# Moving the start addresses of activations, h and shared K/V against the weights in a two-layer decoder trunk

## The chip, the core and the metric

The kernel runs on one core of one Trainium2 chip. The metric is device microseconds of one execution, the median of three runs. A profile is one further execution, recorded by the hardware profiler; its span, from the first to the last instruction, is a little shorter than its own device time.

## What is computed

Two layers of a decoder trunk over 256 positions of width 1024, batch 1, float32. The products that matter are these (cut from the reference):

```python
def swiglu(h, w_in, w_out):
    gu = h @ w_in
    g, u = jnp.split(gu, 2, axis=-1)
    return (jax.nn.silu(g) * u) @ w_out          # D_FF = 2816

def reference(x, c, ...):
    for layer in range(2):
        ...
        x = x + 0.5 * (1.0 + g)[:, None, :] * swiglu(h, ffn_w_in[layer, 0], ffn_w_out[layer, 0])
        ...
        # layer 0: causal pooling mixer; layer 1: block attention on shared K/V
        x = x + (1.0 + g)[:, None, :] * y
        ...
        x = x + 0.5 * (1.0 + g)[:, None, :] * swiglu(h, ffn_w_in[layer, 1], ffn_w_out[layer, 1])
        if layer == 0:
            kv = shared_kv(x, ...)
    return x
```

Ahead of each block stand an RMS norm and a shift and scale that are computed from `c` with the `ada` weights. There are four such SwiGLU blocks in all, and they hold nearly all of the multiplications.

## The kernel before

**Layout.** Channels lie on the 128 partitions, positions run along a row. `xT` holds the residual stream as 8 channel tiles of 256 positions. A float32 product is made of three TensorE matmuls in the format `F32R`: each factor is cut into a high part and the rest (`hi`, `lo` for weights, `hhi`, `hlo` for the normed input h, `acth`, `actl` for the SwiGLU activations, `hkvh`, `hkvl` for the normed input of the shared K/V), and `mm3` (L255 to L260) adds high times high (L256), high weights times low input (L259), and low weights times high input (L260):

```python
    def mm3(o, wh, wl, xh, xl, start, stop):
        i = nc.tensor.matmul(o, wh, xh, start=start, stop=False, skip_group_check=True)
        nc.tensor.matmul(o[:, 0:T], wh, xl, start=False, stop=False, skip_group_check=True)
        nc.tensor.matmul(o, wl, xh, start=False, stop=stop, skip_group_check=True)
```

Each of these loads 128 x 128 weights (the weight load, PEld in the profile, is an instruction of its own) and streams 256 columns of the other factor, the moving operand. A weight block is 512 bytes of each partition's row, a moving operand 1024 bytes. So within one tile every weight block starts at the same address modulo 512, and so does every moving operand, with one exception: the tiles `xah` and `xal` (a scaled copy of `xT` that stands in for h in the first steps of three of the blocks) and `kh`, `kl` (the keys, in the same room) have rows of 258 columns per channel tile, 1032 bytes, so that their k-th piece begins 8k bytes further on.

**Stages.** Weights stream from HBM into `raw` tiles, ScalarE makes `hi` (L168), VectorE makes `lo` (L169), TensorE uses them once. In a SwiGLU block, `gstep` makes one 128-channel piece of gate and up (48 matmuls into `gu`), `evac` turns it into `acth` and `actl`, and `ystep` multiplies these into `y` (24 matmuls for each piece). The projections of K and Q go to `pj`, those of V to `v` (where hkv is the stationary operand and the weights move), scores to `s`, the weighted values to `att`, the output projection to `y` with h as the moving operand. VectorE also makes the modulation vectors with dot products (L264).

**What sets the order.** TensorE's and SyncE's instructions stand in the order in which the program issues them, which lists of steps write out by hand (`MIXER`, `AFTER_B`, `ATTENTION`); the other engines are ordered by a scheduler.

**What sets the addresses.** Six pools are laid one behind another in each partition, in the order of their creation (L91 to L96; `pp` is in PSUM): `ax` (activations), `cp` (constants, `xT`, `mb`, and the rooms `kxhi` and `kxlo`, which hold `xah`, `xal`, `kh`, `kl`), `wp` (weights: `raw`, `hi`, `lo`), `tp` (temporaries), `hp` (h), and behind them `xp` (early tiles of ada weights) and later, in the same place, `ap` (shared K/V, q, probabilities). A tile takes its bytes rounded up to 32. Three tiles are never read or written and only take room: `room0` in `ax`, `room1` in `cp`, `room2` in `hp` (L100, L101, L110). Before, they take 64, 64 and 128 bytes per partition.

Of the kernel before, what the change touches and what calls it, by code (L numbers as in the profile page):

```python
# [7 lines left out]
F32 = mybir.dt.float32  # L8
# [5 lines left out]
P = 128  # L14
# [72 lines left out]
def trunk(ctx: ExitStack, tc: tile.TileContext, xin, cin, small, ada, kvada, win0a, win1a, win0b,  # L87
# [3 lines left out]
    ax = ctx.enter_context(tc.tile_pool(name="ax", bufs=8))  # L91
    cp = ctx.enter_context(tc.tile_pool(name="cp", bufs=1))
    wp = ctx.enter_context(tc.tile_pool(name="wp", bufs=2))
    tp = ctx.enter_context(tc.tile_pool(name="tp", bufs=2))
    hp = ctx.enter_context(tc.tile_pool(name="hp", bufs=1))
# [1 line left out]
    ctx.enter_context(tc.manual_schedule(engines=ORDERED))  # L97


    ax.tile([P, 16], F32, tag="room0", name="room0", bufs=1)  # L100
    hp.tile([P, 32], F32, tag="room2", name="room2")  # L101

    uid = [0]

# [2 lines left out]
        return f"{s}_{uid[0]}"  # L107


    cp.tile([P, 16], F32, tag="room1", name="room1")  # L110
    ident = cp.tile([P, P], F32, tag="ident", name="ident")
    ones = cp.tile([P, P], F32, tag="ones", name="ones")
    sm = cp.tile([P, C_N], F32, tag="sm", name="sm")
# [1053 lines left out]
```

## Time and profile before

| what | value |
|---|---|
| median of three runs | 892.27 us (892.19 to 893.82) |
| the profiled execution, device time | 894.87 us |
| its span | 893.0 us |
| TensorE busy in the span | 881.7 us, 99% |
| VectorE busy | 717.5 us, 80% |
| ScalarE busy | 453.3 us, 51% |
| granted TensorE clock | full (2.4 GHz) throughout |

A matmul's record lasts about 280 ns, because it runs from the start of its stream to the end of its way through the array; the next one starts long before that. So the duration says nothing of the pace. The pace is the distance from one matmul's start to the next one's, called a step here: a stretch of the trace divided by the matmuls that start in it. A count of matmuls in a window takes in those that reach over its ends, which for a record of 0.28 us is two more than start in it.

### The profile page before, as it was taken

Reading aid. Unit: us, or ns where it says so; the run is one execution under the profiler, and the core shown is the slowest. Engines: PE = TensorE matmul, PEld = TensorE weight load, DVE = VectorE, ACT = ScalarE, POOL = GpSimd, SP = SyncE. Lnnn points to the kernel's source line nnn. Section 1 sums busy time; section 2 is a strip of 40 time slices with the busy share of each in tenths; the row PEclk is TensorE's granted clock in tenths of the full one; section 3 lists DMA queues with packets and bytes.
Section 4 is the critical chain, followed back from the end, with each engine's and each line's share of the span. In section 5 each row is a group of like instructions: output and inputs, shape, how many; then the busy total and the mean of one; then the engine's idle time right before and its main releaser. Section 6 shows DMA issues by size and latency. Waiting matters only on the chain.

```text
span 893.0 us, 17812 instructions
## 1 busy us (share of the span) xinstructions
PE 881.7 (99%) x7398; PEld 875.0 (98%) x7398; DVE 717.5 (80%) x1224; ACT 453.3 (51%) x721; POOL 32.3 (4%) x41
## 2 busy tenths in 40 slices
PE   6999999999999999999999999999999999999998
PEld 4999999999999999999999999999999999999998
DVE  5988988878997888869998888779888794665553
ACT  3456444328744343547554434457676584443431
POOL 0000000002000000000000000002211100000000
PEclk9999999999999999999999999999999999999999
DMA  9987998784799998775779989754534277656421
GB/s 353 420 342 270 418 386 346 296 318 160 261 421 417 369 357 337 261 262 183 301 269 385 362 324 359 293 189 142 178 106 132 90 285 276 229 173 202 176 72 48
DMA packets 41699, 240.32 MB, mean 269 GB/s; under 512 B 4625, under 2 KB 5009, under 8 KB 20370
## 3 DMA queue, kind: packets, MB, share of 16 engines
q1 hardware_dynamic: 41618, 239.18, 71.3%
q8 instruction: 58, 0.95, 0.4%
q14 instruction: 23, 0.19, 0.1%
HBM read 238.11 MB, written 1.05 MB: 268 GB/s over the span
## 4 chain that ended last, share of the span: by engine, by line
PE 98%; DVE 1%; ACT 1%; DMA 0%; POOL 0%; issue 0%; DVEq 0%; SPq 0%; POOLq 0%
PE gu L259 18%; PE gu L260 18%; PE gu L256 18%; PE y L259 10%; PE y L260 10%; PE y L256 10%; PE pj L256 2%; PE pj L259 2%; PE pj L260 2%; PE gu L727 1%; PE v L256 1%; PE v L260 1%; PE v L259 1%; PE z L803 1%; PE hs L914 1%; DMA xT<-in_x_dram 0%
## 5 line engine op out<-in xcount | busy, mean ns | idle before, releaser
L168 ACT CAST hi<-raw 128x1024 fp32r<-128x1024 f32 (+1 forms) x322 | 302.5, 974 | 311.6 <-PE gu L259 211.7
L169 DVE TENSOR_TENSOR lo<-raw,hi 128x1024 fp32r<-128x1024 f32 (+1 forms) x322 | 354.6, 1128 | 123.6 <-ACT hi L168 120.8
L259 PE MATMUL gu<-hlo,hi 128*128 128x256 f32 x1248 | 348.6, 279 | 0.0
L260 PE MATMUL gu<-hhi,lo 128*128 128x256 f32 x1248 | 348.4, 279 | 0.0
L256 PE MATMUL gu<-hhi,hi 128*128 128x256 f32 x1248 | 347.9, 279 | 0.0
L260 PEld LDWEIGHTS gu<-hhi,lo 128*128 128x128 f32 x1248 | 234.6, 188 | 0.2 <-DVE lo L169 0.2
L256 PEld LDWEIGHTS gu<-hhi,hi 128*128 128x128 f32 x1248 | 234.6, 188 | 0.0
L259 PEld LDWEIGHTS gu<-hlo,hi 128*128 128x128 f32 x1248 | 234.5, 188 | 0.0
L259 PE MATMUL y<-actl,hi 128*128 128x256 f32 x704 | 196.7, 279 | 0.0
L260 PE MATMUL y<-acth,lo 128*128 128x256 f32 x704 | 196.5, 279 | 0.0
L256 PE MATMUL y<-acth,hi 128*128 128x256 f32 x704 | 196.1, 279 | 0.0
L256 PEld LDWEIGHTS y<-acth,hi 128*128 128x128 f32 x704 | 132.4, 188 | 0.0
L260 PEld LDWEIGHTS y<-acth,lo 128*128 128x128 f32 x704 | 132.3, 188 | 0.0
L259 PEld LDWEIGHTS y<-actl,hi 128*128 128x128 f32 x704 | 132.3, 188 | 0.0
L264 DVE CUSTOM_DVE_ANT_0 rawX<-rawX,cb 128x1024 f32<-128x1024 f32 x88 | 104.1, 1219 | 0.1
L417 ACT ACTIVATE sl<-gu 128x256 f32<-128x256 f32 x79 | 29.4, 377 | 38.3 <-PE gu L260 36.0
L129 ACT CAST acth<-sl 128x256 fp32r<-128x256 f32 x79 | 31.9, 406 | 24.4 <-DVE sl L418 22.6
L418 DVE TENSOR_TENSOR sl<-gu,sl 128x256 f32<-128x256 f32 x79 | 32.8, 418 | 12.7 <-ACT sl L417 12.7
L256 PE MATMUL gu<-xah,hi 128*128 128x258 f32 x144 | 41.3, 287 | 0.0
L260 PE MATMUL gu<-xah,lo 128*128 128x258 f32 x144 | 40.7, 283 | 0.0
L259 PE MATMUL gu<-xal,hi 128*128 128x256 f32 x144 | 40.7, 283 | 0.0
L130 DVE TENSOR_TENSOR actl<-sl,acth 128x256 fp32r<-128x256 f32 x79 | 32.9, 418 | 2.1 <-ACT acth L129 2.1
(147 smaller groups left out, 975.1 us busy)
## 6 DMA issues: line engine op xcount, KB each, us to landing
raw<-in_win1b_dram SPq DMA_DIRECT2D x57, 1024.0 KB, 5.4
raw<-in_wout_dram SPq DMA_DIRECT2D x88, 512.0 KB, 6.0
rawX<-in_ada_dram SPq DMA_DIRECT2D x38, 1024.0 KB, 8.0
raw<-in_win1a_dram SPq DMA_DIRECT2D x14, 1024.0 KB, 9.9
kxhi<-in_ada_dram SPq DMA_DIRECT2D x11, 1024.0 KB, 8.3
raw<-in_win0b_dram SPq DMA_DIRECT2D x12, 768.0 KB, 5.5
kxlo<-in_ada_dram SPq DMA_DIRECT2D x9, 1024.0 KB, 8.4
rawA<-in_ada_dram SPq DMA_DIRECT2D x9, 1024.0 KB, 7.5
```

The costliest lines, as they stand in the source:

```text
L129: i = nc.scalar.copy(hi, src)
L130: nc.vector.tensor_tensor(lo, src, hi.bitcast(F32), op=ALU.subtract)
L168: return [(lambda a=a, b=b: after_anchor(nc.scalar.copy(hi[:, a:b], raw[:, a:b])), lambda a=a, b=b: nc.vector.tensor_tensor(lo[:, a:b], ra ...
L169: lambda a=a, b=b: nc.vector.tensor_tensor(lo[:, a:b], raw[:, a:b], hi[:, a:b].bitcast(F32), op=ALU.subtract)) for a, b in cut]
L256: i = nc.tensor.matmul(o, wh, xh, start=start, stop=False, skip_group_check=True)
L259: nc.tensor.matmul(o[:, 0:T], wh, xl, start=False, stop=False, skip_group_check=True)
L260: nc.tensor.matmul(o, wl, xh, start=False, stop=stop, skip_group_check=True)
L264: i = nc.vector.tensor_tensor_reduce(out=v, in0=v, in1=cb, scale=1.0, scalar=0.0, op0=ALU.mult, op1=ALU.add, accum_out=mb[:, col:col + 1])
L417: nc.scalar.activation(sl, ps[:, 0:T], AF.Silu)
L418: nc.vector.tensor_mul(sl, ps[:, T:2 * T], sl)
L727: nc.tensor.matmul(g0[j][:, half * T:(half + 1) * T], w0[:, (2 * j + half) * P:(2 * j + half + 1) * P], h0, start=(half == 0), stop=False, ...
L803: nc.tensor.matmul(zps[g][:, t * T:(t + 1) * T], xs[:, kt, t * P:(t + 1) * P], pw[:, kt * T:(kt + 1) * T], start=(t == 0 and i == 0), stop ...
```

## The change

The three unused tiles are resized: `room0` goes, `room1` in `cp` grows from 64 to 416 bytes, `room2` in `hp` shrinks from 128 to 32.

```diff
@@ trunk
-    ax.tile([P, 16], F32, tag="room0", name="room0", bufs=1)
-    hp.tile([P, 32], F32, tag="room2", name="room2")
+    hp.tile([P, 8], F32, tag="room2", name="room2")
...
-    cp.tile([P, 16], F32, tag="room1", name="room1")
+    cp.tile([P, 104], F32, tag="room1", name="room1")
```

No instruction is added, removed or moved. In the two built programs every engine has the same instructions in the same order, with the same shapes, the same offsets inside their tiles and the same waits. What differs is where the tiles begin. `ax` moves down by 64 bytes, everything from `cp` through `tp` up by 288, `hp` and what lies behind it up by 192. The starts in each partition, modulo 512:

| tile | before | after |
|---|---|---|
| weights `hi`, `lo`, `raw` | 416 | 192 |
| activations `acth`, `actl` | 192 | 128 |
| `hhi`, `hlo`, `hkvh`, `hkvl`, `qh`, `ql`, `ph`, `pl` | 448 | 128 |
| `xah`, `kh`, piece k | 288 + 8k | 64 + 8k |
| `xal`, `kl`, piece k | 352 + 8k | 128 + 8k |

The phase of a matmul is, in what follows, the start of its moving operand less the start of its stationary one, modulo 512:

| matmuls | phase before | phase after |
|---|---|---|
| `gu` from h, `pj` from hkv and from h, `y` from h | 32 | 448 |
| `y` from the activations | 288 | 448 |
| `gu` from `xah`, piece k | 384 + 8k | 384 + 8k |
| `gu` from `xal`, piece k | 448 + 8k | 448 + 8k |
| `v` (weights move, hkv stands) | 480 | 64 |
| `s` from `kh`, head k | 352 + 8k | 448 + 8k |
| `s` from `kl`, head k | 416 + 8k | 0 + 8k |
| `att` (probabilities move, V stands) | 256 | 0 |

## Rows read from the trace of the kernel before

**Rows 1.** The page: busy us and instructions of each engine, then the chain's engines.

```profile
PE 881.7 (99%) x7398; PEld 875.0 (98%) x7398; DVE 717.5 (80%) x1224; ACT 453.3 (51%) x721; POOL 32.3 (4%) x41
...
PE 98%; DVE 1%; ACT 1%; DMA 0%; POOL 0%; issue 0%; DVEq 0%; SPq 0%; POOLq 0%
```

**Rows 2.** What TensorE waited for: us in total, times, longest.

```profile
PE cb L639 <- DMA crow<-in_c_dram: 2.3, 1, 2.3
PE rb L350 <- POOL r L344: 2.0, 1, 2.0
PE gu L727 <- ACT h L724: 1.5, 1, 1.5
PE ss L336 <- DVE sq L699: 1.2, 1, 1.2
PE att L259 <- DVE pl L130: 0.2, 1, 0.2
```

**Rows 3.** TensorE in stretches of the four SwiGLU blocks: window, length, busy (matmuls), granted clock.

```profile
40.00:200.00 160.00, 160.00 (x1374) 1.00 0.87 341
240.00:400.00 160.00, 160.00 (x1361) 1.00 0.90 349
420.00:580.00 160.00, 160.00 (x1373) 1.00 0.86 326
730.00:880.00 150.00, 150.00 (x1288) 1.00 0.53 187
```

**Rows 4.** Page and tile rows: how many matmuls of each kind there are.

```profile
L256 PE MATMUL gu<-hhi,hi 128*128 128x256 f32 x1248 | 347.9, 279 | 0.0
L256 PE MATMUL y<-acth,hi 128*128 128x256 f32 x704 | 196.1, 279 | 0.0
L256 PE MATMUL y<-hhi,hi x64: 277/280/366, 671.4 to 702.3; 128*128 128x256 f32 x64
L256 PE MATMUL pj<-hkvh,hi x64: 277/278/366, 593.9 to 625.9; 128*128 128x256 f32 x64
L256 PE MATMUL pj<-hhi,hi x64: 277/280/364, 626.2 to 660.8; 128*128 128x256 f32 x64
L256 PE MATMUL v<-hi,hkvh x64: 277/281/369, 588.2 to 668.4; 128*128 128x256 f32 x64
```

**Rows 5.** Timeline, first V step and first `pj` step behind it: start us, us.

```profile
588.20 0.28 PE L256 MATMUL v<-hi,hkvh 128*128 128x256 f32 x1
...
593.89 0.28 PE L256 MATMUL pj<-hkvh,hi 128*128 128x256 f32 x1
```

**Rows 6.** Timeline, six `att` matmuls, from the first to what follows.

```profile
661.13 0.28 PE L256 MATMUL att<-ph,acth 128*128 128x256 f32 x1
...
661.84 0.38 PE L990 MATMUL pT<-ident,p 128*128 128x128 f32 x2
```

**Rows 7.** Timeline, steps from `xah` and `xal`, pieces 0 and 1 in turn.

```profile
214.60 0.28 PE L259 MATMUL gu<-xal,hi 128*128 128x256 f32 x1
...
218.82 0.28 PE L256 MATMUL gu<-xah,hi 128*128 128x258 f32 x1
```

**Rows 8.** Chain of waits: four transposes, whose moving operand has 128 columns.

```profile
612.46 0.44 PE rbk L350 x4
```

**Rows 9.** Timeline, four steps of a K projection and the next start.

```profile
611.24 0.28 PE L256 MATMUL pj<-hkvh,hi 128*128 128x256 f32 x1
611.36 0.28 PE L259 MATMUL pj<-hkvl,hi 128*128 128x256 f32 x1
611.48 0.28 PE L260 MATMUL pj<-hkvh,lo 128*128 128x256 f32 x1
611.60 0.28 PE L256 MATMUL pj<-hkvh,hi 128*128 128x256 f32 x1
611.71 0.28 PE L259 MATMUL pj<-hkvl,hi 128*128 128x256 f32 x1
```

**Rows 10.** VectorE in the stretch that has most of it: window, length, busy.

```profile
420.00:580.00 160.00, 142.81 (x228) 1.00 0.86 326
```

**Rows 11.** VectorE's dot products by source tile: duration ns min/median/max, starts.

```profile
L264 DVE CUSTOM_DVE_ANT_0 rawX<-rawX,cb x88: 1214/1219/1226, 9.2 to 439.7; 128x1024 f32<-128x1024 f32 x88
L264 DVE CUSTOM_DVE_ANT_0 kxhi<-kxhi,cb x24: 1205/1218/1224, 260.8 to 797.5; 128x1024 f32<-128x1024 f32 x24
L264 DVE CUSTOM_DVE_ANT_0 kxlo<-kxlo,cb x22: 1207/1220/1223, 267.3 to 825.5; 128x1024 f32<-128x1024 f32 x22
```

## The prediction

> **What bounds the kernel now.** I read the page first, then what TensorE waited for, then its pace stage by stage. TensorE is busy in 99% of the span and makes 98% of the chain that ended last [rows 1]. All of its waits together are 7.2 us, and all but 0.2 of that lies in the opening, before its first long run of matmuls [rows 2]. So from then on there is one queue of matmuls that never runs dry, and the time is the number of matmuls times the distance between two starts. VectorE has 80% of the span [rows 1], 142.8 of 160 us where it has most [rows 10]; ScalarE has half. The granted clock is full in every stretch [rows 3].
>
> The pace is what the change can touch, so it has to be read finely. In three of the four SwiGLU blocks a step takes 160 us / (1374 - 2) = 116.6 ns, 160 / 1371 = 116.7 and 150 / 1286 = 116.6; in the second block it is 160 / 1359 = 117.7 ns [rows 3]. Nothing waits in any of these stretches, the shapes are equal, and the clock is equal. The V projection goes slower still: 48 steps from 588.20 to 593.89 are 118.5 ns each [rows 5]. The transposes, where the same 128 x 128 weight load goes with only 128 moving columns, come every 0.44 / 4 = 110 ns [rows 8]. So a step of 256 columns costs about 7 ns over what its weight load alone sustains, and how much over depends on something that is neither shape nor wait. What the V projection has of its own is its phase: its moving operand begins 480 bytes beyond the stationary one, not 32 or 288. Phases 32 and 288 both give 116.6.
>
> A rule of the Trainium skill speaks against all this: "TensorE: Matmul & The Clock Gate", section "Step-by-step: what each phase is for", says that weights and moving operand come through read ports of their own, so that loading the next weights takes no read bandwidth from the matmul that runs. By it the start addresses could not matter and the sum would be zero; the rows above show steps that differ by 2 ns among equal shapes, so here it does not settle the question, and it is a rival below.
>
> **The change, part by part.** *Instructions:* none is added or removed and none moves, so nothing is paid or saved there.
>
> *How many steps change their phase.* From 32 to 448: `gu` from h, three lines of 1248; `pj`, three of 64 and three of 64; the output projection, three of 64. From 288 to 448: `y` from the activations, three of 704 [rows 4]. That is 3 x (1248 + 128 + 64 + 704) = 6,432 steps, of which 1,359 lie in the stretch that runs at 117.7 and, for this sum, 5,073 at 116.6 [rows 3]. The steps from `xah` and `xal` (432) keep their phase. V (192) goes from 480 to 64, `att` (48) from 256 to 0, `s` (48) shifts; these 288 have no row at their new phase. They run at about 118.5 now; with 116.6 and 120.6 as ends, both read below, they are worth 288 x -1.9 = -0.5 to 288 x 2.1 = +0.6 us, and I take zero.
>
> *What a step costs at 448.* No row shows a run of equal steps at 448. The nearest are three. V, at 480, is 32 bytes away, and all three matmuls of an `mm3` have the one phase, as they will after the change: 118.5 ns [rows 5]. `att`, at 256, which like 448 is a multiple of 64 while 32, 288 and 480 are not: 0.71 us / 6 = 118.3 ns [rows 6]. The first steps from `xah` and `xal`, where one matmul of every six stands at exactly 448 and the rest between 384 and 456: 4.22 us / 35 = 120.6 ns, part of it because two of three stream 258 columns [rows 7]. On the other side, the transposes' 110 ns [rows 8] is the lowest that a 128 x 128 weight load has here. So the bounds are 110 and 120.6 ns. I take V's 118.5: it is nearest in phase and the only long run in which all steps share one phase that is not 32 or 288, and `att` says the same.
>
> *The sum.* 5,073 x (118.5 - 116.6) = 9.6 us, and 1,359 x (118.5 - 117.7) = 1.1 us: 10.7 us, all of it on the path, since TensorE waits for nobody and a slower TensorE finds every operand earlier. The profiled execution took 894.9 us, so 905.6 by its own time; the median of the runs shown is 2.6 below it, so 903.0 against 892.3. With 120.6 for every step it is 5,073 x 4.0 + 1,359 x 2.9 = 24.2 us: 916.5.
>
> *The other engines.* ScalarE, VectorE and the DMAs read and write at new addresses too. The rows that would show a price are the dot products, which read two tiles at once: from `rawX`, `kxhi` and `kxlo`, which lie 288, 128 and 192 bytes beyond `cb`, they take 1219, 1218 and 1220 ns [rows 11]. After the change the three lie 192, 128 and 192 beyond it. So nothing; and what there was would be covered by TensorE, which reaches its work later than it is ready. That cover is thinnest at 142.8 of 160 us [rows 10].
>
> **The rivals.**
>
> *448 is as good as 32 and 288.* These two are 256 apart and give the same 116.6 [rows 3], so a phase is not simply good or bad by its distance; 448 may be a third of that kind. For it: two of the two phases with thousands of steps agree to 0.1 ns. Against it: every other phase in the trace, 480, 256 and 384 to 504, costs more [rows 5, 6, 7]. It gives 892.3, with 1.5 us less if the second block falls into the pace of the others, 1,359 x 1.1. The rule of ports in the Trainium skill's "TensorE: Matmul & The Clock Gate", told above, would end here too.
>
> *448 is better: the side that is not slower.* The mechanism would be that the weight load's reads and the stream's reads get in each other's way for less of the step. The place is every one of the 6,432 steps; it decides at 116.4 ns, where the sum is 0.2% below. For it: in a K projection at phase 32 steps of 0.12 and of 0.11 us follow each other in a group of four that takes 0.47 us [rows 9], so single steps do get through sooner, and 110 ns is possible for the load [rows 8]. Against it: the four together are no faster than 117, and no phase in the trace holds a lower mean. Half way to 110, at 113.3, it would be 5,073 x 3.3 + 1,359 x 4.4 = 22.7 us: 869.6. All the way, at 110, it is 5,073 x 6.6 + 1,359 x 7.7 = 43.9 us: 848.4. VectorE would then have its 142.8 us in 160 x 110 / 116.6 = 151 us, tight but still not the bound.
>
> *The slow pace of the second block everywhere.* The second block's steps have the phases of the others and are 1.1 ns longer, from its beginning to its end [rows 3]: so there is a state that a run of matmuls enters and keeps. If 448 is neither better nor worse but favours that state in all blocks, it costs 5,073 x 1.1 = 5.6 us: 897.9. This is a smaller slowdown by another cause, and it shows as 117.7 instead of 118.5.
>
> *The change does not do what it says:* the start addresses follow from the tile sizes, and the phases above from them; I give this no weight.
>
> **How the numbers follow.** The forecast, a step of more than 118 ns at 448, gets 0.41; the slow pace everywhere 0.14; as good as before 0.17; better 0.28. A difference of 0.2%, 1.8 us, is about what a measurement of this kernel can tell from none; 10.7 and 5.6 us are well beyond it, so slower is 0.55, same 0.17, faster 0.28. The predicted time is 903.0. The likeliest case alone runs from 899 to 916.5. The range has to hold eight in ten: upward to 916, where all steps cost what the mixed ones do, and downward through the rival that is better to about its half-way price, 872; below that I leave about one in ten, and above the range as many.
>
> **What would show it.** In the changed kernel's trace, the same 160 us stretches hold about 160 / 0.1185 + 2 = 1,352 matmuls if the forecast is right, 1,361 for the slow pace, 1,373 if nothing changed, and over 1,376 if 448 is better. The steps from `xah` and `xal` keep their phase and should keep their 120.6 ns; if they move as well, it is the absolute address and not the phase that counts. The `pj` and output projection steps should have the pace of the `gu` steps, since all share one phase now. TensorE's waits should stay near 7 us; if they grow, the faster pace has run into VectorE. The prediction is wrong if the steps at 448 are at or under 116.6 ns: then nearness of phase, on which I chose 118.5, is no guide.

## The result: a little faster, in two groups of times

The changed kernel takes 890.8 us, median of 11 runs (884.4 to 892.2), against 892.6 for the kernel before (11 runs, 892.2 to 894.5); the ratio is 0.9946, with a 95% interval of 0.9925 to 0.9966. So it is faster by half a percent, inside the range that was given and on the other side of the forecast. The 11 times fall into two groups: five from 884.4 to 885.4 and six from 890.8 to 892.2, with nothing between. The profiled execution is one of the first group: 885.4 us, span 883.5.

The page of the changed kernel, the lines that answer to [rows 1]:

```profile
PE 872.2 (99%) x7398; PEld 865.4 (98%) x7398; DVE 717.1 (81%) x1224; ACT 452.9 (51%) x721; POOL 32.3 (4%) x41
...
PE 97%; DVE 1%; ACT 1%; DMA 0%; issue 0%; POOL 0%; DVEq 0%; SPq 0%; POOLq 0%
```

TensorE's busy time fell by 9.5 us, VectorE's and ScalarE's by 0.4 each: what changed is the pace of the matmuls and nothing beside it. What TensorE waited for stands as in [rows 2], all of it but the last row in the opening:

```profile
PE cb L638 <- DMA crow<-in_c_dram: 2.3, 1, 2.3
PE rb L349 <- POOL r L343: 2.0, 1, 2.0
PE gu L726 <- ACT h L723: 1.5, 1, 1.5
PE ss L335 <- DVE sq L698: 1.1, 1, 1.1
PE att L258 <- DVE pl L129: 0.2, 1, 0.2
```

The pace in stretches of the four SwiGLU blocks of the changed kernel (window, length, busy and matmuls, granted clock), to be read beside [rows 3]:

```profile
30.00:190.00 160.00, 160.00 (x1414) 1.00 0.90 354
230.00:380.00 150.00, 150.00 (x1326) 1.00 0.93 364
415.00:575.00 160.00, 160.00 (x1361) 1.00 0.86 326
710.00:870.00 160.00, 160.00 (x1361) 1.00 0.52 185
```

The first two blocks run at 160 / 1412 = 113.3 and 150 / 1324 = 113.3 ns a step, the last two at 160 / 1359 = 117.7. Before it was 116.6, 117.7, 116.7 and 116.6. At their old paces the same steps would have taken 164.6 us (1412 x 116.6) and 155.8 us (1324 x 117.7) in the first two stretches, and 158.5 (1359 x 116.65) in each of the other two: -4.6, -5.8, +1.5 and +1.5 us, together -7.4 of the 9.5 us; the rest lies in the ends of the blocks and in the projections. So phase 448 does not have one pace. It has two, one better than any before and one worse than most of those before, and in this profile each holds through a whole block, across every change between gate-and-up and y in it.

The distance between the two groups of times, 6 us, is what one block makes: some 1,400 steps x 4.4 ns = 6.2 us. That the slower group has three blocks at 117.8 where this profile has two is an inference; a profile shows one execution. One run below, with three slow blocks, took 891.4 us, which fits.

### The profile page after: what moved, and what is told of

Same layout as the page of the kernel before. It is cut to its first block, busy times and chain, and to the rows that moved or that the text cites. A ratio compares the mean times of both kernels' runs of the same rounds, so it can differ in the third digit from the quotient of the medians.

```text
span 883.5 us, 17812 instructions
## 1 busy us (share of the span) xinstructions
PE 872.2 (99%) x7398; PEld 865.4 (98%) x7398; DVE 717.1 (81%) x1224; ACT 452.9 (51%) x721; POOL 32.3 (4%) x41
## 4 chain that ended last, share of the span: by engine, by line
PE 97%; DVE 1%; ACT 1%; DMA 0%; issue 0%; POOL 0%; DVEq 0%; SPq 0%; POOLq 0%
PE gu L255 18%; PE gu L259 18%; PE gu L258 18%; PE y L259 10%; PE y L255 10%; PE y L258 10%; PE pj L255 2%; PE pj L258 2%; PE pj L259 2%; PE gu L726 1%; PE v L255 1%; PE v L258 1%; PE v L259 1%; PE z L802 1%; PE hs L913 1%; DMA xT<-in_x_dram 0%
## 5 line engine op out<-in xcount | busy, mean ns | idle before, releaser
L259 PEld LDWEIGHTS gu<-hhi,lo 128*128 128x128 f32 x1248 | 237.1, 190 | 0.1
L263 DVE CUSTOM_DVE_ANT_0 rawX<-rawX,cb 128x1024 f32<-128x1024 f32 x88 | 104.2, 1221 | 0.1
```

Of the source, the lines that this page charges most:

```text
L263: i = nc.vector.tensor_tensor_reduce(out=v, in0=v, in1=cb, scale=1.0, scalar=0.0, op0=ALU.mult, op1=ALU.add, accum_out=mb[:, col:col + 1])
```

## One part alone: does each step have its own pace?

Only the sizes of the unused tiles differ (`room1` and `room2`, in floats: 104 and 8 in the changed kernel).

```diff
# h448_act288: h, shared K/V and q at 448, activations at 288
-    cp.tile([P, 104], F32, tag="room1", name="room1")
+    cp.tile([P, 16], F32, tag="room1", name="room1")
# h32_act448: activations at 448, h, shared K/V and q at 32
-    hp.tile([P, 8], F32, tag="room2", name="room2")
+    hp.tile([P, 32], F32, tag="room2", name="room2")
```

> Only h, shared K/V and q begin 448 beyond the weights; the activations keep 288. If each step's pace is set by its own phase, gate-and-up steps take 113.3 and y steps 116.7 ns, 4,100 x 3.3 = 13 us below before where they are in the faster pace, about 880 us. If the pace is a state of the whole stream that both phases must allow, the alternation of 48 and 24 steps holds 117.8 (or 116.7) throughout, 892 to 899 us.

> Only the activations begin 448 beyond the weights; h, shared K/V and q keep 32. If each step's pace is its own, y steps take 113.3 and the rest 116.7 ns: 2,112 x 3.3 = 7 us below before, about 885 us. If the pace is a state of the whole stream, 892 to 899 us.

They took 882.9 and 887.4 us (before: 892.9). The timeline of the first, at the beginning of the third block, with only the first start of each unit (24 y steps, or 48 gate-and-up steps, in a row):

```profile
424.66 0.28 PE L255 MATMUL y<-acth,hi 128*128 128x256 f32 x1
...
427.46 0.28 PE L255 MATMUL gu<-hhi,hi 128*128 128x256 f32 x1
...
433.11 0.28 PE L255 MATMUL y<-acth,hi 128*128 128x256 f32 x1
...
435.92 0.28 PE L255 MATMUL gu<-hhi,hi 128*128 128x256 f32 x1
...
441.37 0.28 PE L255 MATMUL y<-acth,hi 128*128 128x256 f32 x1
```

The first gate-and-up unit takes 5.65 us / 48 = 117.7 and the next 5.45 / 48 = 113.5, and so it stays to the end of the block, while y at 288 takes 2.80 / 24 = 116.7 throughout. In the other kernel the same stretch gives gate-and-up at 32 (443.27 - 437.67) / 48 = 116.7 and y at 448 (446.01 - 443.27) / 24 = 114.2:

```profile
437.67 0.28 PE L255 MATMUL gu<-hhi,hi 128*128 128x256 f32 x1
...
443.27 0.28 PE L255 MATMUL y<-acth,hi 128*128 128x256 f32 x1
...
446.01 0.28 PE L255 MATMUL gu<-hhi,hi 128*128 128x256 f32 x1
```

So each step does have the pace of its own phase, as the first of the two expectations had it. What neither expectation had: where 448 alternates with 288 or with 32, its 117.8 does not last. The third and fourth blocks, slow in the changed kernel, begin slow here as well; gate-and-up leaves the slow pace after its second change to y, and y at 448 (117.8 in its first unit of these blocks) after its first change to gate-and-up. This fits that changing h alone, with fewer steps at 448, beat the full change by 2.5 us (one run against 885.4).

## A map of phases

Again only the sizes of the unused tiles differ.

```diff
# room1, room2 in floats
-  104,  8      # all at 448
+   40, 72      # all192
+   56, 40      # h64_act128
+   32, 48      # h96_act224
+   88, 64      # h160_act0
```

> All three phases at 192 instead of 448 (unused tiles of 160 and 288 bytes). If the phase counts modulo 256, as 32 and 288 suggested, the steps are 113.3 or 117.8 ns as at 448, and the time 873 to 895 us. If it counts modulo 512, another pace appears, and 448 is a place of its own.

> A map of phases, each step's pace taken to be its own: gate-and-up at 64, y at 128. Theory so far: V stood at 64 in the changed kernel and ran at 117.8 in all of its four runs, so gate-and-up should take 117.8; for 128 no row exists, 113 to 121. Time by 117.8 for both about 899 us. If the pace went with distance from 448 both would be equal.

> Gate-and-up at 96, y at 224. V at 480, which is 224 modulo 256, ran at 118.4 before: y should take 118.4. For 96 no row exists. With 118.4 for both about 903 us; under 113 ns in either would make it the better place.

> Gate-and-up at 160, y at 0. The six-matmul runs of the weighted values stood at 0 in the changed kernel and at 256 before, at 118 to 120: y should take 118 to 120. For 160, 32 bytes beside 192, no row exists; if neighbours are alike it is near 113.3. Time 880 to 905 us.

They took 891.4, 898.8, 910.2 and 903.7 us. The four stretches with everything at 192:

```profile
30.00:190.00 160.00, 160.00 (x1361) 1.00 0.87 340
230.00:380.00 150.00, 150.00 (x1322) 1.00 0.92 361
415.00:575.00 160.00, 160.00 (x1361) 1.00 0.86 326
710.00:870.00 160.00, 160.00 (x1360) 1.00 0.55 195
```

These are the same two paces as at 448, 117.7 and (in the second block, but for its beginning) 113.3, dealt out otherwise: here the first block is slow. With gate-and-up at 64 the opening of the first block, before any y step, has 312 matmuls in 35 us, 113 ns; from the first y at 128 on, gate-and-up stays at 117.7 (5.65 us / 48) and y at 118.7 (48 steps in 5.70 us):

```profile
30.00:65.00 35.00, 35.00 (x312) 1.00 0.95 392
```

```profile
499.68 0.28 PE L255 MATMUL y<-acth,hi 128*128 128x256 f32 x1
...
505.38 0.28 PE L255 MATMUL gu<-hhi,hi 128*128 128x256 f32 x1
...
511.03 0.28 PE L255 MATMUL y<-acth,hi 128*128 128x256 f32 x1
```

So a change to another phase can also throw a run out of the fast pace. The other two kernels, one gate-and-up and one y unit each (gate-and-up at 96: 5.76 / 48 = 120.0, y at 224: 2.84 / 24 = 118.3; then y at 0: 2.88 / 24 = 120.0, or 119.8 by the 48 steps from 503.01 to 508.76 us, and gate-and-up at 160: 5.63 / 48 = 117.3):

```profile
441.05 0.28 PE L255 MATMUL gu<-hhi,hi 128*128 128x256 f32 x1
...
446.81 0.28 PE L255 MATMUL y<-acth,hi 128*128 128x256 f32 x1
...
449.65 0.28 PE L255 MATMUL gu<-hhi,hi 128*128 128x256 f32 x1
```

```profile
443.46 0.28 PE L255 MATMUL y<-acth,hi 128*128 128x256 f32 x1
...
446.34 0.28 PE L255 MATMUL gu<-hhi,hi 128*128 128x256 f32 x1
...
451.97 0.28 PE L255 MATMUL y<-acth,hi 128*128 128x256 f32 x1
```

The paces seen, in ns a step:

| phase | paces | where |
|---|---|---|
| 192, 448 | 113.3 and 117.8 | whole blocks of two kernels |
| 64 | 113 and 117.7 | gate-and-up, before and after the first y at 128 |
| 32, 288 | 116.7 and 117.8 | before |
| 160 | 117.3; 118.6 (423.50 to 434.89 us, 96 steps) | gate-and-up; as the third block begins |
| 224, 480 | 118.3, 118.5 | y; V before [rows 5] |
| 128 | 118.7 | y |
| 256, 0 | 118.3, 119.8 | `att` before, six steps [rows 6]; y |
| 96 | 120.0 | gate-and-up |

Neighbours are not alike: 448 and 480, 32 bytes apart, hold 113.3 and 118.5. Phases that differ by 128 or 256 bytes share both their paces in the rows of 64, 192 and 448, and 32 and 288 do; 96 and 224, or 32 and 160, do not agree as exactly. That 160 might be like its neighbour 192 did not come true. The expectations for 0 and 224 held, and that for 64 from the first y on; by 118.4 for both, the kernel with 96 and 224 was expected at 903 us, and 96 made it 910.2.

## What ends the slow pace?

A first attempt put a matmul of one column, whose result nobody reads, ahead of the first gate-and-up piece of the last three blocks:

```diff
+            def kick():
+                o = psum("m", "kick")[:, 0:1]
+                nc.tensor.matmul(o, ident, ones[:, 0:1], start=True, stop=True, skip_group_check=True)
+
             def first_g():
+                kick()
```

> The changed kernel with one more matmul of a single column, about 0.1 us, on TensorE ahead of the first gate-and-up piece from h in each of the last three SwiGLU blocks; its output is not read. Theory, entry decides: at phase 448 a run of steps holds either 113.3 or 117.8 ns, whichever it fell into at its start, and keeps it until the stream is interrupted; after a single-column matmul the K and Q projections fell into 113.3 each time, so all blocks should now run at 113.3: two blocks of about 1,400 steps gain 4.4 ns each, about 12 us below the changed kernel's 885 us runs, 872 to 874 us. Rival, place decides: the last two blocks are slow because of what the other engines and the DMAs do in them; then their 117.8 stays and the time is 885 to 892 us.

It changed nothing: 888.9 us, median of 10 runs, again in two groups, 885.1 to 886.5 and 891.4 to 892.4, and in the profile the last two blocks stayed at 117.7 (1361 matmuls in 160 us). So an interruption of that kind does not decide, and the theory that a short single-column matmul leads into the fast pace fell.

What a block falls into at its start stays open. In the changed kernel the second block, a fast one, begins with a short halt: two steps of 0.19 and 0.22 us, which TensorE's waits do not show, since the records of 0.28 us overlap them. Behind them the pace is 113.3; the last two blocks begin without one and are slow:

```profile
227.57 0.28 PE L258 MATMUL gu<-hlo,hi 128*128 128x256 f32 x1
227.76 0.38 PE L259 MATMUL gu<-hhi,lo 128*128 128x256 f32 x1
227.98 0.29 PE L255 MATMUL gu<-hhi,hi 128*128 128x256 f32 x1
```

A halt alone is not the answer either: the kernel before has one at the same place (0.27 and 0.22 us from 232.50 us on), and there the second block is the slow one; and of the three blocks of `kick448` behind the same extra matmul one was fast and two were slow. In `all192`, near the end of the second block, a single step of 0.16 us (at 392.97 us) has 113.3 ns ahead of it and 117.8 behind it, without any change of phase.

What had ended the slow pace with one part alone was a visit to another phase, that is, one unit of steps there. So in the next kernel two of the eight activation buffers stand 160 bytes lower against the rest, so that the y steps which read them are at phase 288, and the other y and gate-and-up steps stay at 448:

```diff
-    def new_act():
-        return (ax.tile([P, T], F32R, tag="acth", name=nm("acth"), bufs=8),
-                ax.tile([P, T], F32R, tag="actl", name=nm("actl"), bufs=8))
+    def new_act(j):
+        tag, n = ("act%s0", 2) if j % 8 < 2 else ("act%s", 6)
+        r = tuple(ax.tile([P, T], F32R, tag=tag % k, name=nm("act" + k), bufs=n) for k in "hl")
+        if not gap:
+            gap.append(ax.tile([P, 40], F32, tag="room0", name="room0", bufs=1))
+        return r
# few288: in the last three blocks only j < 2
```

> The changed kernel, but two of the eight activation buffers (those of pieces 0, 1, 8, 9, 16 and 17 of each block) begin 288 bytes beyond the weights, so that 24 of 88 y pieces per pass through the four blocks run at phase 288. Theory, the 117.8 ns pace is kept only as long as the phase stays the same modulo 256, and a visit to another phase ends it: all blocks should fall into 113.3 within the first pieces and be thrown back into it twice more; 24 visits cost about 0.1 us each. From 885 with two blocks slow: -12 + 2.4 + about 1 for the slow beginnings, 874 to 878 us, and the two groups of times close up. Rival, the last two blocks are slow because of what the other engines do there: they stay at 117.8, 887 to 894 us.

> As the kernel with two shifted activation buffers, but in the last three blocks only pieces 0 and 1 use them: 12 visits to phase 288 instead of 24. If one pair of visits at a block's start is enough, since the faster pace is kept once it is there, the blocks stay at 113.3 to their end and each visit saved gives back 0.1 us: 876 to 878 us. If a block falls back into 117.8 by itself, it is about 884.

`two288` took 878.1 us, median of 4 runs (875.3 to 879.0); its ratio to the kernel before is 0.981 (0.979 to 0.983). `few288` took 874.9 us, median of 4 (874.3 to 876.7), ratio 0.9794 (0.978 to 0.981). The third block of `two288` at its beginning:

```profile
426.92 0.28 PE L256 MATMUL gu<-hhi,hi 128*128 128x256 f32 x1
...
432.57 0.28 PE L256 MATMUL y<-acth,hi 128*128 128x256 f32 x1
...
435.37 0.28 PE L256 MATMUL gu<-hhi,hi 128*128 128x256 f32 x1
...
440.82 0.28 PE L256 MATMUL y<-acth,hi 128*128 128x256 f32 x1
```

The first of these lines stands right behind the first visit. Between the two visits gate-and-up is at 5.65 / 48 = 117.7, behind the second at 5.45 / 48 = 113.5. In `few288` nothing visits another phase after that, and the last two blocks have 160 / 1406 = 113.8 as the mean of the stretch, in which the slow beginning is still counted:

```profile
415.00:575.00 160.00, 160.00 (x1408) 1.00 0.87 332
710.00:870.00 160.00, 160.00 (x1408) 1.00 0.52 183
```

The rival, that the last two blocks are slow because of what the other engines do there, falls: VectorE, ScalarE and the DMAs do the same work there, and the blocks run fast. And the pace is a state that can last: in each of these two blocks the two visits at the start are enough for the 1,250 steps or so to its end.

## What is being read

Two kernels let the 48 matmuls of each gate-and-up piece read one operand from a single column; what they compute is said in the expectations.

```diff
# weights_one_column
-                    mm3(ps[...], w[0][:, c0:c0 + P], w[1][:, c0:c0 + P],
+                    mm3(ps[...], w[0][:, c0:c0 + 1].to_broadcast([P, P]),
+                        w[1][:, c0:c0 + 1].to_broadcast([P, P]),
# moving_one_column
-                        h[0][:, kt, :], h[1][:, kt, :], ...
+                        h[0][:, kt, 0:1].to_broadcast([P, T]), h[1][:, kt, 0:1].to_broadcast([P, T]), ...
```

> The changed kernel with the stationary operand of the 48 matmuls of each gate-and-up piece from h read from one column, repeated 128 times; so gate and up are not the reference's. Theory, the reads of the weight load and of the stream get in each other's way where they fall into the same part of the memory: with a weight load that stays at one address the step changes clearly, most likely to about 109 ns, the transposes' pace, in which the weights stood at one column too: 3,700 x 4 to 8 = 15 to 30 us. Rival, the pace is set by something in TensorE that has nothing to do with what is read: gate-and-up stays at 113.3 or 117.8.

> The changed kernel with the moving operand of the 48 matmuls of each gate-and-up piece from h read from one column, repeated 256 times; so gate and up are not the reference's. Theory of the two reads: the stream no longer runs through the memory, so at most an eighth or so of the conflicts is left, or all of them if the one place is hit: about 109 ns, or a clearly different pace that does not alternate between 113.3 and 117.8. Rival: 113.3 or 117.8.

Both expectations missed in part. With the weights at one column the pace is 113.3, not 109: 150 / 1324 in three blocks, and in all four:

```profile
30.00:190.00 160.00, 160.00 (x1415) 1.00 0.89 354
230.00:380.00 150.00, 150.00 (x1326) 1.00 0.93 365
410.00:560.00 150.00, 150.00 (x1326) 1.00 0.89 340
710.00:860.00 150.00, 150.00 (x1326) 1.00 0.54 190
```

The slow pace was gone from the four blocks, in y as well, whose operands are untouched (872.5 us, one run). With the moving operand at one column gate-and-up takes (445.72 - 440.36) / 48 = 111.7, and y goes on changing between about 114 ((448.45 - 445.72) / 24) and 118 ((456.64 - 453.81) / 24):

```profile
440.36 0.27 PE L255 MATMUL gu<-hhi,hi 128*128 128x256 f32 x1
...
445.72 0.29 PE L255 MATMUL y<-acth,hi 128*128 128x256 f32 x1
...
448.45 0.27 PE L255 MATMUL gu<-hhi,hi 128*128 128x256 f32 x1
...
453.81 0.28 PE L255 MATMUL y<-acth,hi 128*128 128x256 f32 x1
...
456.64 0.28 PE L255 MATMUL gu<-hhi,hi 128*128 128x256 f32 x1
```

So what TensorE reads does set the pace: with other addresses and the same instructions a step takes 113.3, 116.7, 117.8 or 120 ns, and with a stream of one repeated column 111.7. That the reads of the weight load and of the stream hinder each other would fit the differences above 113.3, since the slow pace did not appear in the blocks of the run where the gate-and-up weights stay in one place. No run shows it directly, and there is a rival: those gate-and-up steps may have ended the slow pace as the visits to 288 do. Nor would two reads in each other's way account for all of the distance to the transposes' 110 ns [rows 8]: 113.3 remains with still weights and 111.7 with a still stream. What the rest is, and which part of the memory the phases count, was not tried.

## A version that tried to gain more

The 432 steps from `xah` and `xal` kept their phase, and their pace. After, first steps from pieces 0 and 1, 35 steps in 4.22 us, 120.6 ns as in [rows 7]:

```profile
209.59 0.28 PE L258 MATMUL gu<-xal,hi 128*128 128x256 f32 x1
...
213.81 0.28 PE L255 MATMUL gu<-xah,hi 128*128 128x258 f32 x1
```

`best` is `few288` with rows of 1152 and 1024 bytes in these tiles. By the sizes, `xal` then stays at phase 448, and the pieces of `xah`, 1152 = 2 x 512 + 128 bytes apart, go through 448, 64, 192 and 320 in turn: one phase only if those four are alike. H, shared K/V and q stand at 320 in this version, and two small tiles were merged into others.

```diff
-        xh = cp.tile([P, KT, T + 2], F32R, tag="kxhi", name=nm("xah"))
-        xl = cp.tile([P, KT, T + 2], F32R, tag="kxlo", name=nm("xal"))
+        xh = cp.tile([P, KT, T + 32], F32R, tag="kxhi", name=nm("xah"))
+        xl = cp.tile([P, KT, T], F32R, tag="kxlo", name=nm("xal"))
```

> The same, and the scaled copies of x and the keys get rows of 1152 and 1024 bytes and start 448 beyond the weights, so their 432 steps keep one phase instead of wandering by 8 bytes; h, shared K/V and q stand at 320, which like 448 is 64 more than a multiple of 128. Theory (64, 192, 320, 448 are alike): those steps fall from 120 to 113.5 to 118 ns, 1 to 3 us, and nothing else changes: 874 to 876 us. If 320 is not like 448, gate-and-up takes 117 or more and the time is above 885 us.

It took 890.6 us, median of 12 runs (887.5 to 893.1), ratio 0.9969 (0.9958 to 0.9981): most of the gain gone. The steps from `xah` and `xal`, expected at 113.5 to 118 ns, took 119.4 in their longest run ahead of the third block (90 in 10.75 us from 404.96 on; in `few288` 10.88 us from 400.57 on, 120.9). In the first block, before any y step, gate-and-up at 320 has 311 matmuls in 35 us, 113 ns, so 320 has the fast pace too. But once y at 448 alternates with it, gate-and-up takes 5.65 / 48 = 117.7 and y 2.73 / 24 = 113.8, and in the last three blocks so it stays:

```profile
30.00:65.00 35.00, 35.00 (x311) 1.00 0.97 396
```

```profile
445.93 0.28 PE L255 MATMUL gu<-hhi,hi 128*128 128x256 f32 x1
...
451.58 0.28 PE L255 MATMUL y<-acth,hi 128*128 128x256 f32 x1
...
454.31 0.28 PE L255 MATMUL gu<-hhi,hi 128*128 128x256 f32 x1
```

In these three blocks each change between 320 and 448, which are 128 apart, throws the stream from one pace into the other: into the slow one at 320, into the fast one at 448. That does not hold everywhere: in the second half of the first block, behind more visits to 288, y at 448 is slow too (48 steps from 158.89 to 164.54 us, 117.7). Changing between 32 and 288, which are 256 apart, never did that before [rows 3]. So 320 and 448 share their paces but not the state. Of the versions that compute the reference, `few288` remains the fastest tried.

## Why the prediction was wrong, step by step

**What bounds the kernel: right.** TensorE waits 7.1 us, the chain is TensorE, and each nanosecond of a step went into the time. Reading the pace as starts in a stretch, and not the duration of 280 ns, was what made the change visible at all.

**Number of steps and the sum's form: right.** 6,432 steps changed their phase. The projections have the same two paces as gate-and-up and y: 48 `pj` steps from 584.14 us on take 117.8 ns each, and 48 from 616.02 us on 113.4. The steps from `xah` and `xal`, whose phase stayed, kept 120.6 ns to the digit while every address under them moved: in this shift it is the difference that counts, the sign that the prediction had named for it.

**What a step costs at 448: the step that failed.** The prediction took V's 118.5 at 480, as the row nearest in phase, and `att` at 256 as a second witness. Both rows were read rightly, 118.5 is V's pace at 480; they say nothing of 448. The map shows that 32 bytes are no nearness: paces go 113.3, 118.5, 119.8 from 448 to 480 to 0. The term came out as -3.3 ns against 116.6 in the first block, -4.4 in the second, and +1.1 in the last two, in place of +1.9 and +0.8 everywhere.

**Two paces for one phase: seen and not used.** The rows before held it: the second block ran at 117.7 where the others, with the same phases, ran at 116.6 [rows 3]. The prediction read this as a state that a run of matmuls enters and keeps, and made of it a rival of its own for the whole kernel. It should have been part of every case: a new phase brings a fast and a slow pace, each block falls into one or the other, and the time is a mixture. With the half-way price of the better rival, 113.3, which is what was measured, in two blocks, and the slow rival's 117.7 in the two others, the prediction's own prices would have given about -8 us. That 113.3 is just the half-way price is luck: half way had no other reason than to lie half way. That the time fell inside the range is no merit of the sum either; the range was wide for the sake of the better rival. Four fast blocks were the 869.6 us of that rival; `few288` comes within 6 us of it, with the blocks' slow beginnings and the visits in its time.

**"No phase in the trace holds a lower mean"** was true and no evidence: the trace held three phases in long runs, 32, 288 and 480, out of the sixteen in steps of 32 bytes, and 32 and 288 are one and the same modulo 256.

**The rest.** The limit of 116.4 ns, at which the better rival was to begin, is a slip: by the prediction's own terms 116.4 is 2.8 us, or 0.3%, below, and 0.2% is reached at about 116.55; nothing hangs on it at 113.3. V at 64 moved from 118.5 to (584.14 - 578.49) / 48 = 117.7, within the ends that were given:

```profile
578.49 0.28 PE L255 MATMUL v<-hi,hkvh 128*128 128x256 f32 x1
...
584.14 0.28 PE L255 MATMUL pj<-hkvh,hi 128*128 128x256 f32 x1
```

VectorE's dot products did not notice the new addresses, 1221 ns against 1219 [rows 11]:

```profile
L263 DVE CUSTOM_DVE_ANT_0 rawX<-rawX,cb x88: 1210/1221/1230, 9.1 to 428.4; 128x1024 f32<-128x1024 f32 x88
```

VectorE did not become the bound at 113.3 either, as the unchanged waits show. What the prediction took from the rule in the Trainium skill's "TensorE: Matmul & The Clock Gate", section "Step-by-step: what each phase is for", by which the next weight load takes no read bandwidth from the matmul that runs, namely that the start addresses could not matter, does not hold in this kernel: with the same instructions and other addresses the step went from 116.6 to 113.3, 117.8 and 120.0 ns, and the measurement decides. Whether read bandwidth is the reason, no run here shows.

## To carry to other kernels

Where TensorE never waits, measure the distance between the starts of equal matmuls, stage by stage: if it differs between stages with the same shapes and no waits, the start addresses of moving and stationary operand are worth a sweep, all phases in steps of 32 bytes, since neighbours tell nothing of each other. Here the phases modulo 256 were the eight to try: those 256 apart agreed within 0.2 ns in long runs (32 and 288, 192 and 448, 224 and 480). Look also for a second pace of the same phase: it shows as a block that is slower as a whole, or as times of one program in two groups. Where there is one, a short visit to another phase early in a long run can end it, and cost a tenth of a microsecond. Which phase does it has to be tried: 288 ended the slow pace at 448, while the first change to y at 128 or 448 put gate-and-up at 64 or 320 into it.

## What was not expected of the hardware

One program, at one phase, holds either of two paces, 113.3 or 117.8 ns a step, through 1,300 steps and more, and an extra matmul of one column ahead of a block does not change which. Two visits of 24 steps to phase 288 did in the last two blocks. A weight load that reads one column leaves the step at 113.3 ns; a stream that reads one column brings it to 111.7.
